# Attention in an encoder layer: two value products for a key tile instead of three, and the sum of the weights added up by DMA

## The chip, the cores and the metric

The kernel runs on one core of a Trainium2 chip. The metric is the time of one execution in microseconds (us). The engines are PE (TensorE, the matrix products), DVE (VectorE), ACT (ScalarE), POOL (GpSimd) and SP (SyncE, which here only issues DMAs). Each engine takes its instructions in the order of its own list and stops at one that has to wait. A DMA that POOL issues goes through the software queue (q0), one from SP through q1, one from ACT through q10; sixteen DMA engines serve all three.

## What is computed

One layer of a bidirectional encoder over a sequence of 2048 tokens and one of 256, with the same weights:

```
n = rmsnorm(x);  p = n @ w_in                          # projections of all mixers
m = mLSTM heads(p), both directions                    # 8 heads of 64
q, k = rope(rmsnorm(q)), rope(rmsnorm(k))              # 8 query heads, 2 key heads
o = softmax(q k^T / 8) v                               # each query sees its whole sequence
x = x + [m; o] @ w_out
x = x + (silu(g) * a) @ w_down,  [a; g] = conv3(rmsnorm(x) @ w_up)
y = rmsnorm(x)
```

The change lies in the line of the softmax. The kernel never normalizes the weights first: it takes w = exp(s - m) for a bound m of each query, sums w·v and w over the keys, and divides at the end.

All of it is float32. A fast product of PE takes operands rounded to a shorter form (the type F32R), so a number a is held as a1 + a2, a rounded part and what is left over, and a product a·b is made of a1·b1 + a1·b2 + a2·b1.

## The kernel before

Tokens stand in tiles of 128; the long sequence has 16 tiles, the short one 2. The program goes through a phase of projections, then attention and mLSTM together, then the output projection (phase C, `po` at L1001), which starts while attention still runs, then the convolution network. A generator for each of attention and mLSTM issues its work in small steps, and `run_both` draws from the one that is behind by a table of costs, so that PE gets both kinds mixed. The order on each engine is then set by the framework's scheduler, which places the instructions by its own times and by priorities; it isn't the order of the Python lines.

**Attention** works through 36 blocks (`hbs`): 32 of one head and 512 queries against the 16 key tiles of the long sequence, and 4 of two heads with 256 queries each against the 2 key tiles of the short one. A block goes through its key tiles two at a time (a pair, `kp`): 8 pairs in a large block, 1 in a small one, 260 in all. For a pair:

- `scores` (L577): four products of 512 columns give s - m for two key tiles in `ps`, a PSUM tile of two banks. ACT takes exp into `pe` (L587) and copies it rounded into the first half of `xx` (L588); DVE puts what is left over into the second half (L589).
- `values` (L592): for each of the two key tiles three products add up in one PSUM bank `pv`, with the keys on the contraction. L600 takes the rounded weights and `vv`, which holds the rounded values in columns 0 to 63 and ones in columns 64 to 127, so rows 64 to 127 of `pv` become the sum of the weights. L601 takes the rounded weights and `vl`, the left-over of the values, into rows 0 to 63. L602 takes the left-over of the weights and `vv`.
- Between pairs, `maxstep` (L548) makes products (`px`, L560) and a maximum on DVE (L562) for the next block's bound m.

After the last pair `fin1` (L604) has ACT copy the value rows of `pv` to `o` and the sum rows to `rs` (L612), and `fin2` (L614) has DVE take the reciprocal and multiply; POOL (SP for the last block) stores the result to `mix_d` (L624), from where phase C loads it (`cmx`, L971). The PSUM tiles `ps`, `px`, `pq` and `pr` share two buffers (tag "sc").

By the constants, `PLAG = 3` lets three pairs of scores be issued ahead of values, `XB = 4` pairs of weights (`xx`) and `PEB = 2` of `pe` have buffers.

**mLSTM on POOL.** POOL also serves mLSTM: it loads rows of gates by DMA (`dm`, L824), masks them (L828), scales keys (`kw`, L793, which the products `mu` of L806 take), and forms inverse roots (`mr`, L97, L98).

## Time and profile before

| what | value |
|---|---|
| median of three runs | 3317.9 us (3312.5 to 3319.42) |
| profiled execution, span from first to last instruction | 3315.5 us |
| attention's products, first scores to last values | 219.7 to 1756.3 us |
| PE busy in the span | 3240.5 us (98%) |
| mean granted clock of PE | 0.992 |
| DMA, mean share of the 16 engines from 222 to 1760 us | 0.38 |

The page gives the span of the profiled execution and no other time of it. A matrix product is in a pipeline, so its duration in a row is longer than the step from its start to the next product's start; what a product takes from PE is read from the starts. In a group's row, the figures behind the count are the group's busy time in us and the mean ns of one; behind the second bar stands how long its engine was idle just before, and what ended that. A row on DMAs gives the size of one and the median us from issue to landing.

### The profile page before, as it was taken

To read this page: it belongs to the slowest core of one execution; us is meant where nothing else is said; L and a number is where in the kernel's file an instruction comes from. 1 tells how busy PE (TensorE), PEld (TensorE's weight loads), DVE (VectorE), ACT (ScalarE), POOL (GpSimd) and SP (SyncE) were. 2 spreads that over 40 slices of the span, in tenths; PEclk is the share of its full clock that TensorE was granted. 3 is DMA by queue.
4 is the path that set the end of the run, shared out by engine and by line. 5 is a ranking of instruction groups with operands and counts; after the bars stand their busy time and mean duration, and the time that the engine had idled before them with its cause. 6 is when DMAs were issued, how large, how long until landed. Compare 5 with 4: busy or idle time off the path is not lost.

```text
span 3315.5 us, 53149 instructions
## 1 busy us (share of the span) xinstructions
PE 3240.5 (98%) x19488; PEld 3018.0 (91%) x19488; DVE 2429.5 (73%) x3759; ACT 1993.5 (60%) x3738; POOL 522.1 (16%) x917
## 2 busy tenths in 40 slices
PE   8989999999999999999999999999999999999998
PEld 7878888888888888788889999999999999999998
DVE  7755676676657768866666899998888889666654
ACT  5646666666675776655454555665676667454543
POOL 4561042223224323200000000000000000020101
PEclk9999999999999999999999999999999999999999
DMA  9973333343346444423227666767676567968663
GB/s 353 316 213 101 112 103 113 98 125 109 99 139 189 123 147 127 139 96 106 76 93 266 220 222 213 248 229 271 202 254 240 194 224 239 320 216 276 216 226 134
DMA packets 359117, 612.31 MB, mean 185 GB/s; under 512 B 31029, under 2 KB 215271, under 8 KB 358855
## 3 DMA queue, kind: packets, MB, share of 16 engines
q1 hardware_dynamic: 329431, 563.14, 50.5%
q0 software_dynamic: 11856, 33.96, 3.8%
q10 hardware_dynamic: 17568, 11.80, 1.1%
q8 instruction: 154, 2.52, 0.3%
q14 instruction: 108, 0.88, 0.1%
HBM read 444.85 MB, written 163.93 MB: 184 GB/s over the span
## 4 chain that ended last, share of the span: by engine, by line
PE 83%; issue 5%; DMA 4%; ACT 3%; DVE 3%; POOL 2%; SPq 1%; POOLq 0%; ACTq 0%; DVEq 0%
PE pa L1164 17%; PE pc L1164 8%; PE pf L1428 7%; PE po L1001 6%; PE pb L1164 4%; PE mj L720 4%; PE pj L238 4%; PE mv L730 4%; PE ph L1428 3%; PE ps L583 3%; PE pv L602 3%; PE pv L600 3%; PE ps L584 3%; PE pv L601 3%; PE px L560 3%
## 5 line engine op out<-in xcount | busy, mean ns | idle before, releaser
L589 DVE TENSOR_TENSOR xx<-pe,xx 128x1024 fp32r<-128x1024 f32 x260 | 319.0, 1227 | 171.4 <-ACT xx L588 169.9
L587 ACT ACTIVATE pe<-ps 128x1024 f32<-128x1024 f32 x260 | 266.1, 1024 | 231.8 <-PE ps L584 215.0
L562 DVE TENSOR_REDUCE mx<-px 128x1 f32<-128x1024 f32 x256 | 310.5, 1218 | 100.6 <-PE px L560 100.0
L588 ACT ACTIVATE xx<-pe 128x1024 fp32r<-128x1024 f32 x260 | 275.1, 1058 | 5.2 <-PE pv L602 0.2
L1381 POOL TENSOR_TENSOR sq<-sq,sq 128x384 f32<-128x384 f32 x38 | 48.5, 1277 | 1382.7 <-ACT sq L1377 1302.2
L1001 PEld LDWEIGHTS po<-cmx,wo 128*128 128x128 f32 x1728 | 229.9, 189 | 19.5 <-DVE cx L1008 1.1
L1001 PE MATMUL po<-cmx,wo 128*128 128x256 f32 x1728 | 238.7, 283 | 1.4 <-DVE cx L1008 1.0
L1168 ACT ACTIVATE u<-pa 128x386 f32<-128x386 f32 (+2 forms) x264 | 128.9, 489 | 173.9 <-PE pa L1164 168.7
L600 PE MATMUL pv<-xx,vv 128*128 128x512 f32 x520 | 212.4, 408 | 10.5 <-ACT rs L612 6.0
L583 PE MATMUL ps<-qq,kk 128*128 128x512 f32 x520 | 213.8, 411 | 8.2 <-ACT pe L587 3.9
L602 PE MATMUL pv<-xx,vv 128*128 128x512 f32 x520 | 211.0, 406 | 3.5 <-DVE xx L589 3.4
L584 PE MATMUL ps<-qm,kl 65*128 65x512 f32 x520 | 208.9, 402 | 0.0
L601 PE MATMUL pv<-xx,vl 128*64 128x512 f32 x520 | 207.3, 399 | 0.0
L720 PEld LDWEIGHTS mj<-mn,wm 128*128 128x128 f32 x1296 | 178.3, 193 | 18.3 <-ACT og L736 4.5
L720 PE MATMUL mj<-mn,wm 128*128 128x256 f32 x1296 | 189.6, 288 | 2.8 <-ACT og L736 2.8
L730 PE MATMUL mv<-wm,mn 128*128 128x256 f32 x1296 | 189.9, 286 | 1.3 <-ACT qb L726 1.3
L730 PEld LDWEIGHTS mv<-wm,mn 128*128 128x128 f32 x1296 | 176.1, 190 | 15.2 <-ACT qb L726 2.3
L238 PE MATMUL pj<-w_a,n1T 128*128 128x512 f32 (+1 forms) x864 | 167.8, 353 | 11.0 <-ACT w_a L105 7.1
L560 PE MATMUL px<-kk,qq 128*128 128x512 f32 x512 | 167.2, 408 | 2.4 <-ACT pe L587 2.4
L238 PEld LDWEIGHTS pj<-w_a,n1T 128*128 128x128 f32 x864 | 141.3, 192 | 30.6 <-ACT w_a L105 7.1
L1164 PE MATMUL pc<-nt,wb 128*128 128x386 f32 (+2 forms) x792 | 148.0, 341 | 0.0
L831 ACT ACTIVATE dm<-dm,tm 128x128 f32<-128x128 f32 x288 | 94.8, 392 | 86.0 <-POOL dm L828 85.7
(337 smaller groups left out, 8106.0 us busy)
## 6 DMA issues: line engine op xcount, KB each, us to landing
mn<-n_d SPq DMA_DIRECT2D x216, 256.0 KB, 3.1
ru<-w_up SPq DMA_DIRECT2D x88, 512.0 KB, 5.1
rs<-wsu_d SPq DMA_DIRECT2D x88, 512.0 KB, 5.7
...
re_t<-wsd_d SPq DMA_DIRECT2D x45, 512.0 KB, 5.4
wsu_d<-tw SPq DMA_DIRECT2D x44, 512.0 KB, 4.2
...
```

Of the source, the lines that this page charges most:

```text
L238: nc.tensor.matmul(pjs[t][:, c0:c1], nTs[tiles[t]][:, c, a, :], ws[c][:, b, c0:c1], start=(c == 0 and k == 0), stop=(c == NCC - 1 and k == 2))
L562: nc.vector.tensor_reduce(s.mx[:, t0, z0:z0 + 1], ps, AX.X, ALU.max)
L583: nc.tensor.matmul(o, kk[:, kc:kc + P], s.qq, start=True, stop=False)
L584: nc.tensor.matmul(o, kl1[:, kc:kc + P], s.qm, start=False, stop=True)
L589: nc.vector.tensor_tensor(x[:, 1], pe, f32(x[:, 0]), ALU.subtract)
L600: nc.tensor.matmul(s.pv, vv[:, kt % 4, :], x1, start=kt == 0, stop=False)
L602: nc.tensor.matmul(s.pv, vv[:, kt % 4, :], x2, start=False, stop=kt == s.nk - 1)
L720: nc.tensor.matmul(pj[:, o].rearrange("p (n t) -> p n t", t=P), s.w[c][:, a, o * P:(o + 1) * P], nT[c][:, :, h, :], start=(c + o + k == 0) ...
L730: nc.tensor.matmul(pv[:, o], nT[c][:, o, a, :], s.w[c][:, h, 256:512], start=(c + o + k == 0), stop=(c == NCC - 1 and k == 2 and o == 1))
L1001: nc.tensor.matmul(po[:, o], wo[c][z // 2][:, a, n], mx[c][:, h, :], start=c + o + k == 0, stop=c == NCC - 1 and o == 1 and k == 2)
L1164: s.nc.tensor.matmul(p, w[:, aa, c, :], ops[k][:, c, bb, 0:s.n], start=c == 0 and i == 0 and not add, stop=c == NCC // 2 - 1 and i == 2, s ...
L1428: nc.tensor.matmul(ps[c], w[:, aa, c, :], t[:, gi - g0, bb, 0:H], start=gi == 0 and m == 0 and not more, stop=gi == NG - 1 and m == 2, ski ...
```

## The change

The value tile `vv` now holds the rounded values in columns 0 to 63 and their left-over in columns 64 to 127, without ones. One product with the rounded weights gives both parts, in rows 0 to 63 and 64 to 127 of `pv`; a second, with the left-over of the weights and the rounded values, adds to rows 0 to 63. The two halves are added in `fin1`. The sum of the weights is no longer made by these products: the first pair's exp goes into a tile of its own, `acc`, and each later pair's `pe` is added to it by a DMA (L603), which POOL issues one pair later; a last DMA (L610) adds the tile's right half to its left half. `fin2` splits that half, `fin3` sums it over the keys with two products against a tile of ones (L651), and `fin4` divides. These steps wait in a list (`later`, `step`) for some pairs. The buffers change: `XB` 4 to 2, `PEB` 2 to 3, `PLAG` 3 to 1, `acc` has two, `o1` two.

```diff
--- before.py
+++ after.py
@@ -1,3 +1,4 @@
+import itertools
 from contextlib import ExitStack
 
 import numpy as np
@@ -69,9 +70,9 @@
 RW = 4
 PO = 4
 PB = 4
-PEB = 2
-XB = 4
-PLAG = 3
+PEB = 3
+XB = 2
+PLAG = 1
 ZT = 3
 SG = 3
 RS = 2
@@ -480,20 +481,17 @@
             s = f"{n}_{t0}"
             kk = sp.tile([P, m * P], F32R, tag="kk" + s, name=f"kk{grp}_{s}", bufs=1)
             kl1 = sp.tile([65, m * P], F32R, tag="kl1" + s, name=f"kl1{grp}_{s}", bufs=1)
-            vv = sp.tile([P, m, P], F32R, tag="vv" + s, name=f"vv{grp}_{s}", bufs=1)
-            vl = sp.tile([P, m, HD], F32R, tag="vl" + s, name=f"vl{grp}_{s}", bufs=1)
+            vv = sp.tile([P, m, 2, HD], F32R, tag="vv" + s, name=f"vv{grp}_{s}", bufs=1)
             c = slice((k0 + t0) * P, (k0 + t0 + m) * P)
             if after is not None:
-                for t in (kk[0:1, 0:1], kk[HD:HD + 1, 0:1], kl1[0:1, 0:1], vv[0:1, 0, 0:1], vl[0:1, 0, 0:1]):
+                for t in (kk[0:1, 0:1], kk[HD:HD + 1, 0:1], kl1[0:1, 0:1], vv[0:1, 0, 0, 0:1]):
                     nc.gpsimd.tensor_copy(t, after[0:1, 0:1])
-            nc.gpsimd.memset(f32(vv[:, :, HD:P]), 1.0)
             for r in (0, HD):
                 nc.gpsimd.dma_start(f32(kk[r:r + HD, :]), g.k_d[grp, 0:HD, c])
             nc.gpsimd.dma_start(f32(kl1[0:HD, :]), g.k_d[grp, HD:P, c])
             nc.gpsimd.memset(f32(kl1[64:65, :]), 1.0)
-            for a, t in ((0, vv[:, :, 0:HD]), (1, vl)):
-                nc.gpsimd.dma_start(f32(t), g.v_d[grp, :, k0 + t0:k0 + t0 + m, a])
-            parts.append((kk, kl1, vv, vl))
+            nc.gpsimd.dma_start(f32(vv), g.v_d[grp, :, k0 + t0:k0 + t0 + m])
+            parts.append((kk, kl1, vv))
 
     class HB:
         pass
@@ -574,6 +572,17 @@
                              stop=True)
         nc.scalar.activation(s.qm[HD:HD + 1, 0:s.N], pr[HD:HD + 1, 0:s.N], AF.Copy)
 
+    due, now, count = [], [0], itertools.count()
+
+    def later(n, f):
+        due.append((now[0] + n, next(count), f))
+        due.sort(key=lambda v: v[:2])
+
+    def step():
+        while due and due[0][0] <= now[0]:
+            due.pop(0)[2]()
+        now[0] += 1
+
     def scores(s, kp):
         kk, kl1 = s.kv[kp // 2][0:2]
         ps = pp.tile([P, 1024], F32, tag="sc", name=f"ps{s.nm}_{kp}")
@@ -582,36 +591,70 @@
             o = ps[:, z * 512:(z + 1) * 512]
             nc.tensor.matmul(o, kk[:, kc:kc + P], s.qq, start=True, stop=False)
             nc.tensor.matmul(o, kl1[:, kc:kc + P], s.qm, start=False, stop=True)
-        pe = sp.tile([P, 1024], F32, tag="pe", name=f"pe{s.nm}_{kp}", bufs=PEB)
+        if kp:
+            pe = sp.tile([P, 1024], F32, tag="pe", name=f"pe{s.nm}_{kp}", bufs=PEB)
+        else:
+            pe = s.acc = sp.tile([P, 1024], F32, tag="acc", name="acc" + s.nm, bufs=2)
         x = sp.tile([P, 2, 1024], F32R, tag="px", name=f"xx{s.nm}_{kp}", bufs=XB)
         nc.scalar.activation(pe, ps, AF.Exp)
         nc.scalar.activation(x[:, 0], pe, AF.Copy)
         nc.vector.tensor_tensor(x[:, 1], pe, f32(x[:, 0]), ALU.subtract)
+        if kp:
+            later(1, lambda: nc.gpsimd.dma_start(s.acc, pe, accum_op=ALU.add))
+        if kp == s.nk // 2 - 1:
+            lo, hi = s.acc[:, 0:512], s.acc[:, 512:1024]
+            n = 2 if kp else 1
+            if s.last:
+                later(n, lambda: nc.vector.tensor_tensor(lo, lo, hi, ALU.add))
+            else:
+                later(n, lambda: nc.gpsimd.dma_start(lo, hi, accum_op=ALU.add))
+            for k, f in enumerate((fin2, fin3, fin4)):
+                later(2 * n + k, lambda f=f: f(s))
         return kp, x
 
     def values(s, kp, x):
 
         if kp == 0:
             s.pv = pp.tile([P, 512], F32, tag="pv", name="pv" + s.nm, bufs=1)
-        vv, vl = s.kv[kp // 2][2:4]
+        vv = s.kv[kp // 2][2]
         for z in range(2):
             kt = 2 * kp + z
             x1, x2 = (x[:, a, z * 512:(z + 1) * 512] for a in range(2))
-            nc.tensor.matmul(s.pv, vv[:, kt % 4, :], x1, start=kt == 0, stop=False)
-            nc.tensor.matmul(s.pv[0:HD], vl[:, kt % 4, :], x1, start=False, stop=False)
-            nc.tensor.matmul(s.pv, vv[:, kt % 4, :], x2, start=False, stop=kt == s.nk - 1)
+            for a in (0, 1) if z == 0 else (1, 0):
+                if a:
+                    nc.tensor.matmul(s.pv[0:HD], vv[:, kt % 4, 0], x2, start=False, stop=False)
+                else:
+                    nc.tensor.matmul(s.pv, vv[:, kt % 4].rearrange("p a d -> p (a d)"), x1, start=kt == 0,
+                                     stop=kt == s.nk - 1)
 
     def fin1(s):
 
-        s.o1 = sp.tile([P, 256], F32, tag="o1", name="o1" + s.nm, bufs=1)
+        s.o1 = sp.tile([P, 256], F32, tag="o1", name="o1" + s.nm, bufs=2)
+        o2 = sp.tile([P, 256], F32, tag="o2", name="o2" + s.nm, bufs=1)
         if s.n == len(hbs) - 3:
             g.hold = s.o1
+        for z in range(2):
+            r, c = slice(HD * z, HD * z + HD), slice(256 * z, 256 * z + 256)
+            nc.scalar.activation(o2[r], s.pv[HD:P, c], AF.Copy)
+            nc.vector.tensor_tensor(s.o1[r], s.pv[0:HD, c], o2[r], ALU.add)
+
+    def fin2(s):
+
+        s.ah = sp.tile([P, 2, 512], F32R, tag="ah", name="ah" + s.nm, bufs=1)
+        nc.scalar.activation(s.ah[:, 0], s.acc[:, 0:512], AF.Copy)
+        nc.vector.tensor_tensor(s.ah[:, 1], s.acc[:, 0:512], f32(s.ah[:, 0]), ALU.subtract)
+
+    def fin3(s):
+
+        ps = pp.tile([P, 1024], F32, tag="sc", name="pa" + s.nm)
+        for a in range(2):
+            nc.tensor.matmul(ps[:, 0:512], g.onesr, s.ah[:, a], start=a == 0, stop=a == 1)
         s.rs = sp.tile([P, 256], F32, tag="rs", name="rs" + s.nm, bufs=1)
         for z in range(2):
-            for r, o in ((0, s.o1), (HD, s.rs)):
-                nc.scalar.activation(o[HD * z:HD * z + HD], s.pv[r:r + HD, 256 * z:256 * z + 256], AF.Copy)
-
-    def fin2(s):
+            r, c = slice(HD * z, HD * z + HD), slice(256 * z, 256 * z + 256)
+            nc.scalar.activation(s.rs[r], ps[r, c], AF.Copy)
+
+    def fin4(s):
         for t in range(2):
             c = slice(t * P, (t + 1) * P)
             nc.vector.reciprocal(s.rs[:, c], s.rs[:, c])
@@ -634,14 +677,13 @@
         yield 0.5
     prep2(cur)
     load_kv(0, 0, NT1, cur.m4)
-    pend, fins = [], []
+    pend = []
 
     def drain():
         b, kp, x = pend.pop(0)
         values(b, kp, x)
         if kp == b.nk // 2 - 1:
             fin1(b)
-            fins.append(b)
 
     for n in range(len(hbs)):
         nxt = prep(n + 1) if n + 1 < len(hbs) else None
@@ -650,7 +692,6 @@
         nkp = cur.nk // 2
         for kp in range(nkp):
             pend.append((cur, *scores(cur, kp)))
-            ready = bool(fins)
             if len(pend) > PLAG:
                 drain()
             if nxt is not None and nxt.todo:
@@ -658,8 +699,7 @@
                     maxstep(nxt)
                 if not nxt.todo:
                     prep2(nxt)
-            if ready:
-                fin2(fins.pop(0))
+            step()
             yield 2.3
         if nxt is not None and nxt.todo:
             while nxt.todo:
@@ -669,8 +709,8 @@
     while pend:
         drain()
         yield 1
-    for b in fins:
-        fin2(b)
+    while due:
+        step()
 
 
 def mlstm(g, tc, s1, sp, sw, sn, pj_, pm):
@@ -1520,6 +1560,8 @@
             sm2 = pool(s_m, "m_o", bufs=2, side="right")
             pm = pool(s_m, "m_p", bufs=MB, space=PSUM, side="right")
             sk = pool(s2, "b_k", bufs=1)
+            g.onesr = sk.tile([P, P], F32R, name="onesr")
+            nc.gpsimd.memset(f32(g.onesr), 1.0)
             sa = pool(s2, "b_s", bufs=2)
             pa = pool(s2, "b_p", bufs=SCB, space=PSUM)
```

The order on POOL, inside mLSTM's second round (`dm` gates, `mr` inverse roots, `kw` scaled keys, `qb` and `va` memsets). Before:

```order
L624 DMA mix_d<-o_0_4739 64x256 [waits DMASW5_49,DVE_49]
L624 DMA mix_d<-o_0_4739 64x256
L824 DMA dm_8_5901<-nm_d 128x512 [waits PE_49]
L828 AFFINE_SELECT dm_8_5901<-dm_8_5901 128x256 [waits DMASW7_49]
L828 AFFINE_SELECT dm_8_5901<-dm_8_5901 128x256
L824 DMA dm_9_6152<-nm_d 128x512 [waits DMASW0_49,DVE_49,PE_49]
L97 TENSOR_SCALAR mr_5_5769<-mms_5_5766 128x2 [waits Activation_49]
L98 TENSOR_TENSOR mr_5_5769<-mr_5_5769,mhalf 128x2 [waits Pool_49]
L828 AFFINE_SELECT dm_9_6152<-dm_9_6152 128x256 [waits DMASW0_49]
L828 AFFINE_SELECT dm_9_6152<-dm_9_6152 128x256
L836 DMA ogr_10_6294<-og_d 128x256 [waits DMAHW7_49,DVE_49]
L725 MEMSET qb_3_4906 64x2x128 [waits PE_49]
```

Now (`acc` is the tile of sums, `pe` a pair's weights):

```order
L603 DMA acc_4_4672<-pe_4_4_4942 128x1024 [waits DMASW1_49,Activation_49]
L864 DMA dm_12_6667<-nm_d 128x512 [waits DMASW3_49,DVE_49,PE_49]
L603 DMA acc_4_4672<-pe_4_5_4988 128x1024 [waits DMASW2_49,Activation_49]
L868 AFFINE_SELECT dm_12_6667<-dm_12_6667 128x256 [waits DMASW3_49]
L868 AFFINE_SELECT dm_12_6667<-dm_12_6667 128x256
L667 DMA mix_d<-o_0_4681 64x256 [waits DVE_49]
L667 DMA mix_d<-o_0_4681 64x256
L98 TENSOR_SCALAR mr_9_6533<-mms_9_6530 128x2 [waits Activation_49]
L99 TENSOR_TENSOR mr_9_6533<-mr_9_6533,mhalf 128x2 [waits Pool_49]
L777 MEMSET va_3_4907 128x4
L833 TENSOR_TENSOR kw_4_6441<-mkt_2_6439,tm 128x256 [waits PE_49]
L876 DMA ogr_14_7085<-og_d 128x256 [waits DMAHW2_49,DVE_49]
```

Two of a block's seven additions stand among mLSTM's steps here; each waits for ACT and for a DMA semaphore of the software queue (DMASW), and the steps behind it are issued after it.

The order on PE around one pair of a large block (`ps` scores, `pv` values, `px` next block's bound, `mv`, `mN`, `mT`, `mt` mLSTM). Before:

```order
L730 MATMUL mv_1_5615<-wm_5_4843,mn_1_5_5549 128x256
L600 MATMUL pv_4_4768<-xx_4_3_4764,vv_16_4_2556 128x512
L601 MATMUL pv_4_4768<-xx_4_3_4764,vl_16_4_2557 64x512
L730 MATMUL mv_1_5615<-wm_5_4843,mn_1_5_5549 128x256
L730 MATMUL mv_1_5615<-wm_6_4844,mn_1_6_5550 128x256 x4
L863 MATMUL mN_7_6122<-va_3_2386,dm_7_5783 128x65 x4
L602 MATMUL pv_4_4768<-xx_4_3_4764,vv_16_4_2556 128x512
L600 MATMUL pv_4_4768<-xx_4_3_4764,vv_16_4_2556 128x512
L601 MATMUL pv_4_4768<-xx_4_3_4764,vl_16_4_2557 64x512
L602 MATMUL pv_4_4768<-xx_4_3_4764,vv_16_4_2556 128x512
L730 MATMUL mv_1_5615<-wm_6_4844,mn_1_6_5550 128x256
L583 MATMUL ps_4_5_4978<-qq_4_4164,kk_16_8_2570 128x512
```

Now:

```order
L592 MATMUL ps_4_4_4937<-qq_4_4169,kk_16_8_2561 128x512
L593 MATMUL ps_4_4_4937<-qm_4_4171,kl_16_8_2562 128x512
L592 MATMUL ps_4_4_4937<-qq_4_4169,kk_16_8_2561 128x512
L593 MATMUL ps_4_4_4937<-qm_4_4171,kl_16_8_2562 128x512
L627 MATMUL pv_4_4720<-xx_4_3_4768,vv_16_4_2551 128x512
L558 MATMUL px_4_2_1_4951<-kk_16_8_2561,qq_4_4662 128x512
L558 MATMUL px_4_2_1_4951<-kk_16_12_2573,qq_4_4662 128x512
L827 MATMUL mt_2_6436<-ident,mkT_2_4902 128x128 x2
L925 MATMUL mT_2_6511<-ident,hh_4_5521 128x128
L925 MATMUL mT_2_6511<-ident,hh_5_5777 128x128
L625 MATMUL pv_4_4720<-xx_4_3_4768,vv_16_4_2551 64x512 x2
L627 MATMUL pv_4_4720<-xx_4_3_4768,vv_16_4_2551 128x512
```

The six value products of a pair, in a group of two and one of four, have become four, in a group of one and one of three; the group of one stands right behind the next pair's scores.

The order on PE behind the last block's values, where phase C's products (`po`) follow. Before:

```order
L600 MATMUL pv_12_19545<-xx_12_7_19739,vv_16_12_10502 128x512
L601 MATMUL pv_12_19545<-xx_12_7_19739,vl_16_12_10503 64x512
L602 MATMUL pv_12_19545<-xx_12_7_19739,vv_16_12_10502 128x512
L1001 MATMUL po_3_20177<-cmx_3_19887,wo_1_17024 128x256 x3
L1001 MATMUL po_3_20177<-cmx_4_19891,wo_1_17050 128x256 x3
L1001 MATMUL po_3_20177<-cmx_5_19895,wo_1_17060 128x256 x3
```

Now (`pa` sums the weights with ones):

```order
L1041 MATMUL po_3_20215<-cmx_3_19929,wo_1_17054 128x256 x3
L1041 MATMUL po_3_20215<-cmx_4_19933,wo_1_17079 128x256 x3
L1041 MATMUL po_3_20215<-cmx_5_19937,wo_1_17089 128x256 x3
L1041 MATMUL po_3_20215<-cmx_6_19941,wo_1_17140 128x256 x3
L1041 MATMUL po_3_20215<-cmx_7_19945,wo_1_17150 128x256 x3
L1041 MATMUL po_3_20215<-cmx_0_19916,wo_1_17009 128x256 x3
L1041 MATMUL po_3_20215<-cmx_1_19921,wo_1_17019 128x256 x3
L1041 MATMUL po_3_20215<-cmx_2_19925,wo_1_17044 128x256 x3
L651 MATMUL pa_12_19853<-ah_12_19850,onesr 128x512 [waits Activation_49]
L1041 MATMUL po_3_20215<-cmx_3_19929,wo_1_17054 128x256 x3
L1041 MATMUL po_3_20215<-cmx_4_19933,wo_1_17079 128x256 x3
L651 MATMUL pa_12_19853<-ah_12_19850,onesr 128x512 [waits DVE_49]
```

Behind the last values phase C's products follow as before; the two products for the sum of the last block's weights, which wait for ACT and DVE, now stand among them, 26 and 32 products behind the last value product.

## The prediction

> **What bounds the kernel now.** I read the head of the page, then the busy times of the stretch that holds attention, then PE in order of time, then the groups with the idle time before them.
>
> ```profile
> span 3315.5 us, 53149 instructions
> 222.00:1760.00 1538.00, 1504.87 (x9468) 1308.97 (x9468) 1048.33 (x1851) 965.31 (x2035) 347.14 (x677) 1.00 0.38 118
> ```
>
> The second row is the stretch from 222 to 1760 us: its length, then busy time of PE, PE's weight loads, DVE, ACT and POOL, then PE's clock (1.00), the share of the DMA engines (0.38) and GB/s. PE is busy 98% of it, DVE 68%, ACT 63%, POOL 23%. A busy PE need not be a full one, since products overlap in its pipeline; so the starts count:
>
> ```profile
> 1743.18 0.40 PE L602 MATMUL pv<-xx,vv 128*128 128x512 f32 x1
> 1743.41 0.39 PE L600 MATMUL pv<-xx,vv 128*128 128x512 f32 x1
> 1743.64 0.40 PE L601 MATMUL pv<-xx,vl 128*64 128x512 f32 x1
> 1743.88 0.39 PE L602 MATMUL pv<-xx,vv 128*128 128x512 f32 x1
> ...
> 1746.69 0.40 PE L601 MATMUL pv<-xx,vl 128*64 128x512 f32 x1
> ```
>
> From the first of these rows to the last are 15 steps from one product of 512 columns to the next, in 3.51 us: 0.234 us a step. The product with 64 output rows (L601) takes the same step as the others (1743.64 to 1743.88). Next, whether PE waits for what it takes:
>
> ```profile
> L583 PE MATMUL ps<-qq,kk 128*128 128x512 f32 x520 | 213.8, 411 | 8.2 <-ACT pe L587 3.9 <-DVE mx L562 2.5 <-ACT qm L575 1.7
> L600 PE MATMUL pv<-xx,vv 128*128 128x512 f32 x520 | 212.4, 408 | 10.5 <-ACT rs L612 6.0 <-ACT xx L588 4.1
> L602 PE MATMUL pv<-xx,vv 128*128 128x512 f32 x520 | 211.0, 406 | 3.5 <-DVE xx L589 3.4
> L560 PE MATMUL px<-kk,qq 128*128 128x512 f32 x512 | 167.2, 408 | 2.4 <-ACT pe L587 2.4
> L601 PE MATMUL pv<-xx,vl 128*64 128x512 f32 x520 | 207.3, 399 | 0.0
> L583 PEld LDWEIGHTS ps<-qq,kk 128*128 128x128 f32 x520 | 98.9, 190 | 29.1 <-ACT pe L587 7.1 <-DVE mx L562 5.4 <-ACT qm L575 2.0
> ```
>
> Attention's products were held 8.2 + 10.5 + 3.5 + 2.4 = 24.6 us in all, in 1538, and none of that by POOL or a DMA. So PE's own work sets the time here, and work taken from PE is worth its steps as long as nobody else becomes late.
>
> The Trainium skill (Trainium Kernel Development and Optimization, Best Practices) calls matmul busy time a bad measure and the busy share of weight loads a good one. By that share, 1309 of 1538 or 85%, PE would have 15% to spare, and if as much of the removed work came out of spare time the saving would shrink by some 16 us. The starts above show products without a gap, at a step longer than a weight load (0.19 us, the last row), so I keep the full step.
>
> **The change part by part.**
>
> *Products.* The 520 products of L601 go: 520 x 0.234 = 121.7 us off PE. The 36 blocks each get two products of 512 columns for the sum of the weights: 72 x 0.234 = 16.8 us on. The other value products keep their number and their columns. Net: -104.9 us, or 0.40 us of a pair's 1538/260 = 5.92 us. A pair then has 5.51 us, a large block of eight pairs 44.1 us.
>
> *ACT and DVE.* The nearest rows for the added work:
>
> ```profile
> L1136 ACT ACTIVATE wd<-ru 128x512 fp32r<-128x512 f32 x66 | 41.0, 623 | 0.0
> L1137 DVE TENSOR_TENSOR wd<-ru,wd 128x512 fp32r<-128x512 f32 x66 | 45.3, 687 | 1.2 <-ACT wd L1136 1.2
> L618 DVE TENSOR_TENSOR o<-o,rs 128x256 f32<-128x256 f32 x36 | 15.0, 418 | 0.3
> ```
>
> ACT splits the sums once a block, 36 x 0.62 = 22 us, and has as many copies out of PSUM as before (two from `pv`, two from `pa`, where it had four from `pv`). DVE gets the left-over of that split, 36 x 0.69 = 25 us, and two additions of the value halves, 72 x 0.42 = 30 us. Over the shortened stretch of 1433 us DVE rises to 1103/1433 = 77% and ACT to 987/1433 = 69%. That lies beside PE's work, but PE now has less to do while it waits for them, and the free share of DVE falls from 32% to 23%. The halving of the buffers of `xx` comes on top. The rows on the order show that PE already took values about one pair behind scores, so `PLAG` itself moves little there. The 24.6 us of waits may stay or take back all 105; I let them nearly double, +22 us, since nothing in the stretch is close to full.
>
> *The additions.* 32 large blocks get seven additions of 512 KB and all but the last block one of 256 KB: 224 + 35 = 259 issues on POOL.
>
> ```profile
> L624 POOL DMA_DIRECT2D mix_d<-o x70 | 38.6, 554 | 355.8 <-ACT xx L588 171.0 <-issue 71.1 <-ACT csq L1011 35.2
> mix_d<-o POOLq DMA_DIRECT2D x70, 64.0 KB, 2.3
> ogr<-og_d POOLq DMA_DIRECT2D x27, 128.0 KB, 2.9
> dm<-nm_d POOLq DMA_DIRECT2D x72, 256.0 KB, 3.7
> rd<-w_down SPq DMA_DIRECT2D x22, 512.0 KB, 3.3
> ```
>
> At 0.554 us an issue POOL gets 143 us more, 490 of 1433 us or 34%. The weight lies elsewhere: the additions of a block go into one tile, so each waits for the landing of the one before, and POOL waits with it. Before has no adding DMA, and none within the chip's own memory. From the rows of POOL's queue, 128 KB more cost 0.8 us, so 512 KB would land after 3.7 + 2 x 0.8 = 5.3 us. From below, SP's row of 512 KB has 3.3. From above, if reading the target costs as much again as reading the source, 5.3 + 4 x 0.8 = 8.5. I take 5.3: it is the row of the same queue carried to this size, with the second read hidden, and it lies between. A block's chain is then 7 x 5.3 + 0.55 for the next issue = 37.7 us; the last addition of 256 KB goes beside the next block's first. That is under 44.1, and `pe` has three buffers, so exp of a pair need not wait until two pairs later. The chain is hidden, with 15% to spare.
>
> The Trainium skill (DMA: Bandwidth & Descriptors, Anatomy of one DMA — SWDGE (gpsimd) path) fits a DMA of this queue as 2.0 us plus its bytes at 436 GB/s, and (Collectives: The Full Stack, The bandwidth ceiling: the fold count and why AG ≠ RS ≠ AR) says that an add must read two sources through one ring. An estimate from both is 2.0 + 2 x 1.2 = 4.4 us, by which the sum would lose only its term for the end, 5 us. The trace's 256 KB row has 3.7 where the fit gives 2.6, so here the queue is slower than the page.
>
> *What waits behind an addition on POOL.* In the order, masks of `dm`, the keys `kw` and the roots `mr` stand behind additions.
>
> ```profile
> POOL dm L828 <- DMA dm<-nm_d: 188.7, 66, 5.1
> POOL kw L793 <- PE mu L806: 169.5, 45, 21.1
> ```
>
> POOL spent 189 us waiting for `dm` to land and 170 for PE to free `kw`, so it ran ahead of PE, with room to be late. A chain of 37.7 us in 44.1 uses up much of this room; `dm` itself now lands behind 512 KB on the same queue. What is late next is `mu` (L806), which takes `kw`, and PE stops there. Nothing (if the room suffices) up to the whole of the rival below; I take 0.3 us a block, +10 us.
>
> *Stores, loads, the end.* Ten loads and ten memsets of the value tiles are saved on POOL, off any path. `fin4` comes some pairs later, so phase C gets `mix_d` later; other tiles cover that until the last block:
>
> ```profile
> 1700.00:1760.00 60.00, 13.73 (x14) 0.97 0.19 60
> ...
> 1756.30 0.39 PE L602 MATMUL pv<-xx,vv 128*128 128x512 f32 x1
> 1756.54 16.21 PE L1001 MATMUL po<-cmx,wo 128*128 128x256 f32 x135
> ```
>
> (the first row counts 14 exps of ACT in 60 us.) There a pair takes 4.3 us, 3.9 after the change, less than an addition's 5.3: the chain falls behind by up to 7 x 1.4 = 10 us. Before, 135 products of phase C followed the last values at 0.12 us each. Now the sum's products stand 26 products, 3.1 us, behind them. Of the 10 us I charge 5; between nothing and, at 8.5, 7 x 4.6 = 32.
>
> *The sum*, on the profiled execution: 3315.5 - 121.7 + 16.8 + 22 + 10 + 5 = 3247.6. The median of the runs stands 2.4 us above that span, so **3250 us**.
>
> **The rivals.**
>
> *The additions set the pace (slower).* Place: POOL, from one addition of a block to the next. As soon as an addition takes over (44.1 - 0.55)/7 = 6.2 us, exp finds no free `pe`, ACT stops, and scores stop behind it; above 6.7 us the saving of 3.3 us a block is gone. For it: the DMA engines already carry 38%, the second read may not hide, mLSTM's waits on POOL add to the chain. Against it: 5.3 from the rows. At 7 us a block takes 49.6, and 32 x (49.6 - 44.1) = 176 us come back: 3315.5 - 104.9 + 176 + 2.4 = 3389; at 8.5 it is 3723.
>
> *The saving goes into waits for ACT and DVE (no change).* With two buffers of `xx`, a late left-over on DVE stops values on PE and the copy on ACT at once. It needs 0.4 us more wait a pair, against 0.1 now: about 3318. Against it: DVE and ACT stay under 80%.
>
> *All of it is kept.* No added wait anywhere: 3315.5 - 104.9 + 2.4 = 3213. Against it: fewer buffers and fuller engines.
>
> **How the numbers follow.** The forecast gets 0.58, all kept 0.08, no change 0.10, the additions' pace 0.24. A measurement of this kernel tells about 0.2% (6.6 us) from no change. Faster: 0.58 + 0.08 = 0.66; the case of no change gives 0.09 to within 0.2% and 0.01 to slower, which makes 0.25. The forecast's own range is 3215 to 3295. For 8 times in 10 the range must take in no change and the near part of the slow rival, an addition of up to about 6.8 us: 3208 to 3350, with 0.03 below and some 0.15 above.
>
> **What would show it right or wrong.** The rows of L603 should land after 4 to 6 us. PE's starts in a pair should keep 0.234, with four value products a pair, and idle time before PE's attention groups near 45 us. PE should not wait for POOL, and ACT's exp not for a DMA. The stretch from first scores to last values should shrink from 1538 to about 1470 us. Landings over 6.2 us, with exp waiting for L603, would be the slow rival; waits of values for DVE of 100 us the second. The stages before 222 us and after phase C should keep their times; a difference there would be something I did not see.

## The result: 8.7% slower, and the profile after

The change takes 3604.4 us in the median of four runs (3596.9 to 3607.0), the kernel before 3317.6 us beside it: a ratio of 1.0866, with a 95% interval of 1.0851 to 1.0882. The forecast was 3250 us. The profiled execution has a span of 3603.0 us, 287.5 more than before.

First the stretch from the first scores to the last values, in the view of busy times by window (length; then busy time of PE, its weight loads, DVE, ACT, POOL; PE's clock, DMA share, GB/s). Before, cut at its last value product:

```profile
222.00:1757.00 1535.00, 1501.87 (x9442) 1305.97 (x9442) 1046.67 (x1849) 964.07 (x2032) 347.14 (x677) 1.00 0.38 118
```

After:

```profile
222.00:2032.00 1810.00, 1534.07 (x8997) 1313.33 (x8996) 1099.87 (x1953) 990.21 (x2067) 550.58 (x916) 0.90 0.69 169
```

The stretch is 275 us longer. PE's idle time in it rose from 1535 - 1502 = 33 to 1810 - 1534 = 276 us, which is 243 more. PE's busy time rose too, by 32 us, though 104.9 us of products were taken from it. The clock column says why: 1.00 before, 0.90 now, so each product takes longer on average; that is worth 32 + 105 = 137 us, an estimate from the two busy times and the prediction's net work. So -105 us of work, +243 of idle time and +137 of lower clock make +275. The other 12 us lie behind the stretch (1571 us after its end, 1558.5 before).

What ended PE's idle time, by groups of instructions:

```profile
L592 PE MATMUL ps<-qq,kk 128*128 128x512 f32 x518 | 228.3, 441 | 33.2 <-ACT pe L599 18.4 <-DVE mx L560 7.6 <-ACT rs L655 6.2
L627 PE MATMUL pv<-xx,vv 128*128 128x512 f32 x520 | 219.4, 435 | 38.3 <-ACT xx L600 33.7 <-DVE o L639 2.9 <-DMA mn<-n_d 1.4
L558 PE MATMUL px<-kk,qq 128*128 128x512 f32 x512 | 183.3, 441 | 71.7 <-ACT pe L599 41.3 <-DVE mx L560 26.7 <-ACT acc L599 1.9
L625 PE MATMUL pv<-xx,vv 128*64 128x512 f32 x520 | 181.4, 427 | 15.7 <-DVE xx L601 15.7
```

PE idles 159 us ahead of these four, 25 ahead of the four of before, and mostly for exp (`pe`) and its rounded copy (`xx`), both on ACT. Neither ACT nor DVE is fuller than before (ACT 990 of 1810 us). So the next question is what stands ahead of exp. The waits of ACT in the stretch, after:

```profile
ACT dm L871 <- POOL dm L868: 186.9, 57, 10.1
ACT pe L599 <- PE ps L593: 161.2, 109, 6.8
ACT ah L644 <- DMA acc<-acc: 116.6, 28, 13.2
ACT qm L573 <- PE pr L571: 68.1, 19, 7.6
ACT cmx L1012 <- DMA cmx<-mix_d: 53.2, 17, 10.2
...
ACT pe L599 <- DMA acc<-pe: 4.6, 2, 3.1
```

and the first two of before:

```profile
ACT pe L587 <- PE ps L584: 214.7, 131, 6.7
ACT dm L831 <- POOL dm L828: 85.7, 57, 4.8
```

ACT waits twice as long for POOL's masks (`dm`), up to 10.1 us at a time; for the last landing of a block's sum before it may split it (`ah`, new, up to 13.2 us); and for `cmx` (13.2 us before). Exp comes behind these in ACT's own order and is late with them, although exp itself hardly waits for a landing (4.6 us). POOL's waits, after:

```profile
POOL acc L603 <- ACT pe L599: 283.8, 67, 10.2
POOL acc L603 <- DMA acc<-pe: 192.3, 50, 7.0
POOL dm L868 <- DMA dm<-nm_d: 119.6, 47, 6.6
POOL acc L610 <- DMA acc<-pe: 103.8, 26, 6.8
```

This view puts 284 us of POOL's waits at additions down to an exp and 192 + 104 us to a landing. But it names whatever last updated one of the semaphores waited for, and ACT updates its own with most of its instructions (1297 of 2066 in the stretch), so an exp can be named by coincidence. The trace has the times to check it: the end of the exp whose weights an addition takes, and the landing of the addition before it. Measured so, 124 of the waits ahead of L603, 509 us together, end about 0.5 us after that landing, and only 64, 262 us, right after the addition's own exp. Of the waits ahead of L610, 124 us end with a landing. POOL thus stands still for landings more than twice as long as for exp. The landings themselves (KB each, median us from issue to landing):

```profile
acc<-pe POOLq DMA_DIRECT2D x224, 512.0 KB, 5.2
dm<-nm_d POOLq DMA_DIRECT2D x72, 256.0 KB, 5.2
acc<-acc POOLq DMA_DIRECT2D x35, 256.0 KB, 3.7
mix_d<-o POOLq DMA_DIRECT2D x70, 64.0 KB, 4.7
```

An addition lands after 5.2 us in the median, where 5.3 was forecast; the mean is 5.5. But the gates `dm` now take 5.2 us (3.7 before) and the stores of `mix_d` 4.7 (2.3 before). They share POOL's queue with the additions, which is only part of the reason: with as many stores going through ACT's queue instead (a run below) they still take 4.5 and 2.8 us.

One block's end shows the whole chain in order of time (start, duration, engine; in brackets the engine's idle time and what ended it):

```profile
1551.75 0.92 POOL L603 DMA_DIRECT2D acc<-pe  x1 [4.05 <-issue]
...
1556.87 0.87 POOL L603 DMA_DIRECT2D acc<-pe  x1 [4.20 <-DMA acc<-pe]
...
1559.06 3.13 PE L1041 MATMUL po<-cmx,wo 128*128 128x256 f32 x25
1562.35 0.85 POOL L610 DMA_DIRECT2D acc<-acc  x1 [4.60 <-DMA acc<-pe]
1566.97 0.63 ACT L644 ACTIVATE ah<-acc 128x512 fp32r<-128x512 f32 x1 [11.58 <-DMA acc<-acc]
...
1568.03 1.02 ACT L599 ACTIVATE pe<-ps 128x1024 f32<-128x1024 f32 x1
...
1569.52 1.22 PE L558 MATMUL px<-kk,qq 128*128 128x512 f32 x2 [7.33 <-DVE mx L560]
```

The block's last two additions and the half addition follow each other by their landings; ACT stops 11.58 us at the split; the next pair's exp, whose scores were issued from 1558 us on, starts at 1568.03; PE has nothing left at 1562.2 and idles 7.33 us. The seven additions of this block began at 1517.87 and the last had landed at 1562.06, after 44 us, where 37.7 were forecast. Three of its earlier additions, and the exp whose weights the last of these takes, show why:

```profile
1531.16 0.86 POOL L603 DMA_DIRECT2D acc<-pe  x1 [4.23 <-ACT xx L600]
...
1533.06 1.03 ACT L599 ACTIVATE pe<-ps 128x1024 f32<-128x1024 f32 x1 [0.26 <-PE ps L593]
...
1539.44 0.86 POOL L603 DMA_DIRECT2D acc<-pe  x1 [7.43 <-issue]
...
1545.74 0.86 POOL L603 DMA_DIRECT2D acc<-pe  x1 [5.43 <-ACT pe L599]
```

The addition at 1545.74 takes weights that were ready at 1534.09; the exp that the view names is a later pair's. By the trace, the addition before it landed at 1544.91. None of this block's seven additions waited for its own exp, which was done 2.5 to 11.7 us ahead: the landings took 4.5 to 7.7 us each, 39.2 us together, and each next start came 0.5 to 2 us behind a landing. The last landing is 14 us behind the block's last exp.

Over all 32 large blocks a chain took 48.3 us in the mean (36.7 to 59.4). Of these, 38.8 us are the seven landings, 3.2 us the half microsecond that lies between a landing and the next addition's start, and 6.4 us later starts, 5.1 of them until the addition's own exp was done.

What follows for PE, in three windows around the same place:

```profile
1562.00:1569.00 7.00, 0.19 (x2) 0.00 (x0) 1.37 (x2) 1.98 (x4) 0.85 (x1) 0.68 0.48 126
1569.00:1573.00 4.00, 3.48 (x9) 2.60 (x10) 3.94 (x8) 3.35 (x9) 0.86 (x1) 0.50 0.60 115
1573.00:1585.00 12.00, 12.00 (x81) 11.17 (x80) 7.00 (x11) 3.87 (x5) 1.56 (x2) 0.93 0.37 89
```

For 4 us behind the idle time the granted clock is 0.50. So this wait is paid for twice. The Trainium skill (TensorE: Matmul & The Clock Gate, What's actually happening) says that the gate passes all or half of the pulses and falls to half after an idle window of some 3.4 us; the 0.50 here agrees.

A second path, through the store of `mix_d`:

```profile
1696.92 0.86 POOL L603 DMA_DIRECT2D acc<-pe  x1 [4.16 <-issue]
1697.45 1.41 POOL L667 DMA_DIRECT2D mix_d<-o  x2
1702.23 0.80 SPq L1011 DMA_DIRECT2D cmx<-mix_d  x2
1704.67 0.83 ACT L1012 ACTIVATE cmx<-cmx 128x256 fp32r<-128x256 f32 x2 [10.14 <-DMA cmx<-mix_d]
...
1705.13 1.26 PE L1041 MATMUL po<-cmx,wo 128*128 128x256 f32 x4 [9.29 <-ACT cmx L1012]
...
1705.52 1.03 ACT L599 ACTIVATE pe<-ps 128x1024 f32<-128x1024 f32 x1
```

The store stands behind an addition on POOL, the load of `cmx` behind the store, ACT behind the load for 10.14 us, and exp behind ACT.

### The profile page after: what moved, and what is told of

Its sections match the earlier page's. It is cut to its first block, busy times and chain, and to the rows that moved or that the text cites. A ratio compares the mean times of both kernels' runs of the same rounds, so it can differ in the third digit from the quotient of the medians.

```text
span 3603.0 us, 53035 instructions
## 1 busy us (share of the span) xinstructions
PE 3276.9 (91%) x19040; PEld 3029.1 (84%) x19040; DVE 2483.6 (69%) x3868; ACT 2017.4 (56%) x3774; POOL 724.6 (20%) x1153
## 5 line engine op out<-in xcount | busy, mean ns | idle before, releaser
L601 DVE TENSOR_TENSOR xx<-pe,xx 128x1024 fp32r<-128x1024 f32 x224 | 275.2, 1230 | 178.5 <-ACT xx L600 170.7
L603 POOL DMA_DIRECT2D acc<-pe x224 | 200.5, 895 | 799.1 <-ACT pe L599 283.8
L599 ACT ACTIVATE pe<-ps 128x1024 f32<-128x1024 f32 x224 | 229.2, 1024 | 167.9 <-PE ps L593 161.2
L627 PE MATMUL pv<-xx,vv 128*128 128x512 f32 x520 | 219.4, 435 | 38.3 <-ACT xx L600 33.7
L558 PE MATMUL px<-kk,qq 128*128 128x512 f32 x512 | 183.3, 441 | 71.7 <-ACT pe L599 41.3
L600 ACT ACTIVATE xx<-pe 128x1024 fp32r<-128x1024 f32 x224 | 236.4, 1057 | 16.6 <-PE pv L627 7.8
L760 PE MATMUL mj<-mn,wm 128*128 128x256 f32 x1296 | 206.5, 306 | 19.2 <-ACT og L776 9.8
L625 PE MATMUL pv<-xx,vv 128*64 128x512 f32 x520 | 181.4, 427 | 15.7 <-DVE xx L601 15.7
L627 PEld LDWEIGHTS pv<-xx,vv 128*128 128x128 f32 x520 | 106.1, 204 | 79.8 <-ACT xx L600 44.2
L558 PEld LDWEIGHTS px<-kk,qq 128*128 128x128 f32 x512 | 92.8, 208 | 94.1 <-ACT pe L599 48.9
```

The costliest lines, as they stand in the source:

```text
L558: nc.tensor.matmul(ps[:, z * 512:(z + 1) * 512], s.qq[:, t0 * P:(t0 + 1) * P], s.kv[2 * z0 + z][0], start=True, stop=True)
L599: nc.scalar.activation(pe, ps, AF.Exp)
L600: nc.scalar.activation(x[:, 0], pe, AF.Copy)
L601: nc.vector.tensor_tensor(x[:, 1], pe, f32(x[:, 0]), ALU.subtract)
L627: nc.tensor.matmul(s.pv, vv[:, kt % 4].rearrange("p a d -> p (a d)"), x1, start=kt == 0, stop=kt == s.nk - 1)
L760: nc.tensor.matmul(pj[:, o].rearrange("p (n t) -> p n t", t=P), s.w[c][:, a, o * P:(o + 1) * P], nT[c][:, :, h, :], start=(c + o + k == 0) ...
```

## The experiments

Ratios are against the kernel before on the same chip, with 95% intervals; a hundredth is 33 us, and a difference of two ratios is known to within some 7 to 12 us. Each run was made from the changed kernel unless it says otherwise. The diffs are shortened to the lines that matter. Where a run leaves out a part of the sums, it also adds a small constant so that the division stays finite. In the runs with additions later, two chains, sums set aside, and POOL emptied, the split's tile `ah` also takes a buffer of `pe`.

**The buffers alone** (in the kernel before):

```diff
-PEB = 2; XB = 4; PLAG = 3
+PEB = 3; XB = 2; PLAG = 1
```

> The kernel before with the change's buffers and lag alone: PEB 3, XB 2, PLAG 1; three products a key tile as before, no additions. Theory A: 3310 to 3350 us. Rival B: 3450 us or more.

3333.3 us, 1.006 [1.0037, 1.0083]. Fewer buffers cost some 19 us with three products; they are not the cause.

**The products alone** (in the kernel before; the sum of the weights is left out, and DVE adds the value halves as in the change):

```diff
-            nc.tensor.matmul(s.pv, vv[:, kt % 4, :], x1, ...)
-            nc.tensor.matmul(s.pv[0:HD], vl[:, kt % 4, :], x1, ...)
-            nc.tensor.matmul(s.pv, vv[:, kt % 4, :], x2, ...)
+            nc.tensor.matmul(s.pv, vv[:, kt % 4].rearrange("p a d -> p (a d)"), x1, ...)
+            nc.tensor.matmul(s.pv[0:HD], vv[:, kt % 4, 0], x2, ...)
```

> Left out: the sum of the weights (no additions, no split, no products with ones; the division takes another row of the value products instead). This is the kernel before with two value products a key tile in place of three and with its own four buffers of xx and values up to three pairs behind: what the removed products alone are worth. Theory 3 (the smaller buffers take the saving: with two buffers of xx values wait for the left-over and PE falls under its full clock): with the deep buffers 104 to 122 us are kept, 3195 to 3225 us, PE's clock 0.99. Theory 4 (PE waits for ACT and DVE whatever the buffers, so the removed work was not worth its steps): 3290 to 3340 us.

> The same with the change's buffers: two of xx, three of pe, values one pair behind. Left out as there: the sum of the weights. Theory 3: 3310 to 3340 us, as the change without its additions (3336). Theory 4: the same as with the deep buffers within 25 us. If it is faster than 3300, the split and the products with ones cost more than I think.

> The same with three buffers of xx, two of pe and values two pairs behind, the sum of the weights left out again. Theory 3: between the two others, 3220 to 3280 us. Theory 4: no difference among the three.

With before's buffers 3266.2 us, 0.9863 [0.9845, 0.9880]; with the change's 3276.4, 0.9893 [0.9877, 0.9909]; with three of `xx` 3260.9, 0.9847 [0.9828, 0.9866]. Neither theory had the times: the three differ by 5 to 16 us, so the buffers matter little, as theory 4 had it; but 35 to 50 us are saved, neither 104 to 122 nor next to nothing. The stretch of the first:

```profile
222.00:1708.00 1486.00, 1417.10 (x8922) 1231.08 (x8923) 1066.09 (x1919) 948.77 (x1959) 335.33 (x655) 0.98 0.40 121
```

Against before, PE's work fell by 122 us and its busy time by 85 (the clock, 0.98, takes 37), and its idle time rose by 36, from 33 to 69. Ahead of attention's products PE now idled 47 us, not 24.6, and nearly all of it ended with an instruction of ACT or DVE: given less to do, PE waits for these two sooner. That the clock fell because of this idle time is a reading, not shown by a run of its own.

**The change without its additions, and with their traffic alone:**

```diff
-            later(1, lambda: nc.gpsimd.dma_start(s.acc, pe, accum_op=ALU.add))
-                later(n, lambda: nc.gpsimd.dma_start(lo, hi, accum_op=ALU.add))
# the second kernel also:
+            nc.scalar.dma_start(g.junk_d[kp], pe)
```

> Left out: all adding DMAs, so the sum of the weights is that of a block's first pair alone; a small constant is added to it so that the division stays finite. Everything else is as in the change, the split, the products with ones and the smaller buffers too. If the additions and the waits for their landings are what costs (theory 1: the two queues that must keep their order, POOL's with the chain of additions and ACT's with the split that waits for the last landing), the time falls to 3220 to 3270 us, the stretch from 222 us on to some 1450 us and PE's clock there is back at 0.99. If something else in the change costs (two buffers of xx, values one pair behind, the sums of value halves on DVE), it stays above 3400 us.

> Left out: the additions, as in the kernel without them; instead ACT's queue stores every pe tile but a block's first to the chip's memory, 224 stores of 512 KB, which nobody reads and for which only the reuse of pe waits. So much of the additions' traffic is there without their order: no chain, no wait on POOL, no split that waits. Theory 1: within 40 us of the kernel without additions, and under 3310 us. Theory 2 (traffic slows loads and stores that others wait for): 3400 us or more.

3335.6 us, 1.0059 [1.0044, 1.0074], and 3343.1 us, 1.0084 [1.0066, 1.0102]. The first lies between its two forecasts (3220 to 3270, or above 3400); the second is within 40 us of it, as theory 1 had it, but not under 3310. Two things follow. The additions cost 1.0866 - 1.0059 = 0.081, 268 us; and without them the change is still slower than before. The kernel with the same products and buffers but no split, no products with ones and no late end stood at 0.9893: these three cost 0.017, 55 us, where 16.8 had been charged for the products of ones. And 224 stores of 512 KB for which only the reuse of `pe` waits cost 8 us, hardly more than the two intervals allow for: traffic of this size is not the cause. These stores read the weights but not the sums, and go through ACT's queue, so what an addition does to POOL's own queue isn't in this run. The stretch without additions, and three windows in it:

```profile
222.00:1778.00 1556.00, 1460.89 (x8987) 1259.80 (x8988) 1096.91 (x1955) 992.62 (x2065) 348.43 (x656) 0.96 0.38 115
```

```profile
1571.00:1575.00 4.00, 0.67 (x4) 0.23 (x3) 4.00 (x6) 0.00 (x0) 0.00 (x0) 0.70 0.75 235
1575.00:1590.00 15.00, 14.74 (x41) 10.66 (x41) 5.17 (x9) 8.44 (x12) 1.09 (x2) 0.51 0.21 61
1590.00:1600.00 10.00, 6.92 (x21) 4.49 (x20) 7.40 (x8) 4.02 (x6) 0.00 (x0) 0.83 0.00 0
```

Here PE idled 95 us in the stretch, and the clock was 0.96. PE's rows where these windows begin:

```profile
1570.32 0.68 PE L621 MATMUL pv<-xx,vv 128*64 128x512 f32 x2 [2.05 <-DVE xx L601]
1570.85 0.63 PE L623 MATMUL pv<-xx,vv 128*128 128x512 f32 x2
1574.80 1.11 PE L621 MATMUL pv<-xx,vv 128*64 128x512 f32 x2 [3.33 <-DVE xx L601]
```

Two waits of 2.05 and 3.33 us are followed by 15 us at half clock, though PE is busy in 14.74 of them. The Trainium skill (TensorE: Matmul & The Clock Gate, What's actually happening) has the full clock back after one busy window of 3.4 us; this place doesn't agree, and the measurement decides.

**Half of each addition:**

```diff
-dma_start(s.acc, pe, accum_op=ALU.add)
+dma_start(s.acc[:, 0:512], pe[:, 0:512], accum_op=ALU.add)
```

> The change with additions of half the size: each of the seven adds only the left 512 columns, so the even key tiles alone are summed (and a small constant is added ahead of the reciprocal). Same count, same chain, half the bytes. If the chain of landings decides, a landing falls from 5.2 to about 3.7 us, a block from 56 us by 7 x 1.5 = 10 us or more, 3250 to 3350 us. If it is POOL's waits as such, whatever their length: 3450 us or more. Rival B: about 3600.

3450.2 us, 1.0408 [1.0378, 1.0438]. This is not the 3250 to 3350 us forecast for the case that the chain of landings decides, but the edge of the other case, that POOL's waits cost as such. Still, the landings take 3.7 us instead of 5.2, POOL's waits that end with a landing ahead of L603 fall from 509 to 230 us by the trace's times, and the cost of the additions falls from 268 to 116 us. So more than half of it goes with the size of an addition, most likely through the length of its landing; 116 us stay with landings this short.

**The split later, and the additions later:**

```diff
# split, products with ones and division three pairs later
-                later(2 * n + k, lambda f=f: f(s))
+                later(2 * n + k + (3 if kp else 0), lambda f=f: f(s))
# the other kernel: additions two pairs later, four buffers of pe, split two pairs later still
-            later(1, lambda: nc.gpsimd.dma_start(s.acc, pe, accum_op=ALU.add))
+            later(2, lambda: nc.gpsimd.dma_start(s.acc, pe, accum_op=ALU.add))
```

> The split, the products with ones and the division of a large block come three pairs later; the additions are untouched, the result is the reference's. Theory 1a (ACT stops at the split until the half addition has landed, 117 us in 28 waits of up to 13 us, and exp stands behind it): those waits go, and with them PE's long idle times and part of the half clock behind them; 3400 to 3480 us. Theory 1b (the chain of additions on POOL alone makes masks, roots and stores late): 3560 to 3610 us. Theory 2 (the traffic of the additions slows every transfer): 3580 to 3610 us.

> Additions are issued two pairs later instead of one, with four buffers of pe instead of three, the half addition one pair later and the split two more pairs behind it (its tile takes a buffer of pe); the result is the reference's. Theory 1 (POOL stops at an addition whose exp is not yet done, 284 us in 67 waits, and ACT at a split whose sum has not landed): both waits go, 3300 to 3420 us. If POOL's stop for exp costs nothing, it is as with the late split alone. Theory 2 (traffic): 3560 us or more.

3570.4 us, 1.0771 [1.0755, 1.0787], and 3528.7 us, 1.0638 [1.0616, 1.0660]. The late split was placed later by the program, yet ACT's waits at it did not shrink (144 us in 31 waits), so it tests its theory only weakly. With the additions later, ACT's waits for a landing at the split did go, from 117 to 15 us. POOL's wait for exp fell from 284 to 144 us by the view (262 to 133 by the trace's times). That for landings rose from 192 us by the view (509 to 578 by the trace's times):

```profile
POOL acc L603 <- DMA acc<-pe: 287.5, 68, 8.2
```

A part of POOL's wait moved from one cause to the other; 76 us were gained, less than the 180 us or more of the forecast.

**Two chains:**

```diff
-dma_start(s.acc, pe, accum_op=ALU.add)
+dma_start(s.acc2 if kp % 2 else s.acc, pe, accum_op=ALU.add)   # joined by one more addition
```

> The change with two tiles of sums, one for even and one for odd pairs, which a last addition joins, so that an addition waits only for the one before the last; the split comes later (its tile takes a buffer of pe). The result is the reference's. Theory 1b (each addition waits on POOL for the landing before it, 197 us, and what stands behind is late): those waits go, 3400 to 3500 us. If POOL's order against ACT's exp is what costs, or the traffic, it stays at 3540 to 3610 us.

3492.7 us, 1.0548 [1.0527, 1.0569]: 105 us gained, as theory 1b had it. POOL's wait for the landing before fell from 192 to 20 us (by the trace's times, from 509 to 4), but 147 us of waiting now lie ahead of the addition that joins the tiles and 116 ahead of the half addition. A new wait came in on ACT too, at the next block's second pair, whose exp needs the second tile back:

```profile
POOL acc L605 <- DMA acc<-pe: 20.1, 6, 4.6
ACT acc L601 <- DMA acc<-acc: 105.0, 23, 10.1
```

**The additions set aside**, into a tile that nobody reads:

```diff
-dma_start(s.acc, pe, accum_op=ALU.add)
+dma_start(g.ad, pe, accum_op=ALU.add)
```

> Left out: the additions go into a tile of their own that nobody reads, so the sum of the weights is that of a block's first pair alone (with a small constant added). POOL issues every addition, the half addition too, in its place and waits as in the change; what falls away is only that ACT's split and the next use of the sums' tile wait for a landing. Without any addition the time is 3336, with all 3604. Theory 1a (ACT's stop at the split is the larger part): 3340 to 3420 us. Theory 1b (POOL's own order, with masks, roots and stores late, is the larger part): 3480 to 3570 us.

3571.4 us, 1.0784 [1.0752, 1.0817]: 240 of the 268 us stay, just above what theory 1b expected. ACT's stop for the sums, plain as it is in the timeline, is worth 27 us alone; 30 us of stops at the split stay in this run, for the buffer of `pe` that its tile takes, so this figure is rather low. The other stops are larger than in the change (187, 94 and 53 us there):

```profile
ACT dm L871 <- POOL dm L868: 210.1, 60, 12.0
DVE hh L917 <- POOL mr L99: 113.4, 44, 7.3
ACT cmx L1012 <- DMA cmx<-mix_d: 69.1, 29, 9.6
```

**The removed work given back:**

```diff
-                    nc.tensor.matmul(s.pv[0:HD], vv[:, kt % 4, 0], x2, ...)
+                    for _ in range(2):
+                        nc.tensor.matmul(s.pv[0:HD], vv[:, kt % 4, 0], x2, ...)
```

> The change with 520 more value products: the product of the weights' left-over is issued twice, so that left-over counts double. PE gets back 520 x 0.234 = 122 us of work, nothing else changes. If PE's work still sets the time in the change: 3690 to 3730 us. Theory 5 (in the change PE stands behind ACT and POOL, and its idle time and its half clock swallow the saving): under 3650 us, with less idle time and a higher clock in the stretch than the 0.90 of the change.

3622.5 us, 1.0928 [1.0906, 1.0949]: 122 us of products cost 18 to 21 us.

```profile
222.00:2056.00 1834.00, 1615.29 (x9518) 1358.81 (x9516) 1103.36 (x1950) 989.63 (x2062) 554.97 (x913) 0.94 0.69 166
```

PE idles 219 us in place of 276 and its clock rises from 0.90 to 0.94. In the change PE's work does not set the time: of work given back, a sixth shows.

**Other adders**: POOL itself, DVE, and DVE for pairs with three DMAs a block:

```diff
# POOL; for DVE nc.vector
-later(1, lambda: nc.gpsimd.dma_start(s.acc, pe, accum_op=ALU.add))
+later(1, lambda: nc.gpsimd.tensor_tensor(s.acc, s.acc, pe, ALU.add))
# pairs: pe1 onto acc by DVE; pe2+pe3, pe4+pe5, pe6+pe7 by DVE, then
+later(1, lambda: nc.gpsimd.dma_start(s.acc, b, accum_op=ALU.add))
```

> The change with every addition made by POOL itself (one instruction over 128 x 1024 in place of a DMA). From 1.28 us for 384 columns an addition takes about 3.4 us; POOL gets 35 + 224 x 3.4 = 800 us of work and no landing to wait for. Theory A: POOL's chain is 7 x 3.4 = 24 us a block, well under 44, so 3230 to 3320 us. Rival B: 3450 us or more. If an addition on POOL slows beside DVE to over 6 us: 3500 or more.

> No adding DMA: DVE adds each pair's weights to the sums, 224 x 1.23 = 276 us, and the halves. The result is the reference's. POOL and ACT wait for no landing. DVE then has some 1380 of 1480 us. If being nearly full is enough to stop PE: 3420 to 3520 us, with values waiting for the left-over on DVE. If DVE keeps up: 3340 to 3380 us. Theory 1 excludes only 3560 and more.

> Three adding DMAs a large block instead of seven: DVE adds the second pair's weights to the sums and joins the others two by two (four additions of 1.2 us), and a DMA adds each joined pair; split, products with ones and division one or two pairs later. The result is the reference's. Theory 1 (the cost goes with the number of landings and stops on POOL): a bit under half of the 269 us of the additions stays, 3400 to 3470 us, if DVE (then some 87% busy) does not stop PE itself; otherwise 3480 to 3550 us.

POOL: 3486.1 us, 1.0516 [1.0486, 1.0547]. DVE: 3418.0, 1.0308 [1.0285, 1.0331]. Pairs: 3456.5, 1.0437 [1.0404, 1.0470]. The first was a miss for theory A, and another cause came in; the third is as theory 1 had it. Additions on POOL, and DVE's left-over beside them:

```profile
L603 POOL TENSOR_TENSOR acc<-acc,pe 128x1024 f32<-128x1024 f32 x224 | 557.9, 2491 | 391.8 <-ACT pe L599 349.3 <-DVE xx L601 20.0 <-DVE C L857 10.3
L601 DVE TENSOR_TENSOR xx<-pe,xx 128x1024 fp32r<-128x1024 f32 x224 | 392.1, 1753 | 112.4 <-ACT xx L600 111.8
```

An addition takes 2.49 us on POOL, and DVE's subtraction rises from 1.23 to 1.75 us; PE's waits for it ahead of L625 rise from 15.7 to 58.5 us. The Trainium skill (GPSIMD Engine Reference, Key points) says that POOL shares its interfaces to SBUF with DVE, with contention when a DVE instruction has two inputs there. The row agrees. With DVE adding, no landing is waited for, and of the additions' 268 us 83 remain: DVE is then busy 1359 of 1638 us, and values wait for it (36.7 us on PE). The time lies at the lower end of the 3420 to 3520 us expected if a nearly full DVE stops PE. Three DMAs a block instead of seven, with their work on DVE, leave 125. None of these comes near the kernel before.

**POOL emptied of mLSTM's work**, with the additions, without them, and with two chains:

```diff
-        nc.gpsimd.dma_start(o.dm..., g.nm_d[...])          # og too
+        nc.sync.dma_start(o.dm..., g.nm_d[...])
-            nc.gpsimd.affine_select(out=o.dm[:, d], ...)
+            nc.vector.tensor_tensor(o.dm[:, d], o.dm[:, d], g.mask[:, d], ALU.add)
-            nc.gpsimd.tensor_tensor(kw, ...)
+            nc.vector.tensor_tensor(kw, ...)
```

> The change with most of mLSTM's work taken off POOL: the gate rows and the output gates are loaded by SP, DVE adds a mask that was made once, DVE scales the keys; POOL keeps the additions, the stores and the inverse roots. The result is the reference's. Theory 1b (what stands behind the additions on POOL is late, and ACT and DVE stop for it): the waits of ACT for masks go (187 us in the change), 3400 to 3500 us. Rival (the chain of landings itself holds exp and the split, whatever else POOL does): 3560 to 3610 us.

> The same moves off POOL without any addition (left out: the additions, so the sum of the weights is that of a block's first pair alone, with a small constant added). It tells what the moves alone do: against the kernel without additions (3336 us) both theories expect 3320 to 3370 us, since ACT's 94 us of waits for masks may shrink and DVE gets 72 masks and 72 scaled keys more, about 80 us of its work. What lies between this run and the one with additions is then the cost of the additions with POOL nearly to themselves: theory 1b 60 to 150 us, the rival 200 us or more.

> The same moves off POOL with the two tiles of sums. The result is the reference's. If both causes are what the runs so far say (work behind the additions on POOL, and each addition's wait for the landing before it), their gains add up in part: 3380 to 3440 us. If the moves bring nothing, 3490 us as with two tiles alone. None of the theories expects a time under that of the kernel before.

3483.1 us, 1.0505 [1.0488, 1.0521]; without additions 3330.0, 1.0044 [1.0029, 1.0059]; two chains 3491.2, 1.0533 [1.0498, 1.0568]. The moves alone do nearly nothing (1.0059 to 1.0044), but with them the additions cost 1.0505 - 1.0044 = 0.046, 153 us, not 268. So 115 us of the additions' cost went through mLSTM's steps that stand behind them on POOL, or through its loads, which no longer take POOL's queue; the run doesn't tell these two apart. On POOL itself the waits for landings ahead of L603 stay (648 us by the trace's times). With both, 3380 to 3440 us were forecast, so that was a miss: the gains of the moves and of the two chains do not add up; with both, ACT still waits 104 us for a join. How the last 153 us divide among the chain's waits, the late `cmx` (76 us on ACT there) and the split was not settled.

## Why the prediction was wrong, step by step

*What bounds the kernel now.* Right for the kernel before. But "work taken from PE is worth its steps as long as nobody else becomes late" is where the saving ended: with the products removed and little else changed, 45 us came of 121.7. In the stretch the loss was 73 us: 36 of new idle time and 37 of clock. The rule on weight loads of the Trainium skill (Trainium Kernel Development and Optimization, Best Practices), set aside since the starts showed no gap, would have taken off some 16 us. It pointed the right way, but fell short. The rival in which the saving goes into waits for ACT and DVE gave 3318 us; without the additions the change takes 3336. That rival was the better forecast of that part.

*ACT and DVE.* The +22 us for doubled waits: without the additions PE idled 95 us in the stretch, 62 more than before, and the lower clock took another 64 (1460.9 busy against 1501.9 - 104.9 = 1397). The two make 126 us, five to six times the term, and half of that is the lower clock, which the prediction put at nothing.

*The additions.* The median landing was right, 5.2 us for 5.3. The step that failed is "The chain is hidden, with 15% to spare". A block's chain took 48.3 us in the mean, not 37.7: the mean landing is longer than the median, half a microsecond lies between a landing and the next start, and some starts were late. Even without the late starts it is 42.0 us, and that would have left 5% of the 44.1, not 15. Above all, the step compared the chain's length with the block's, as if POOL had nothing else in its list. In fact POOL stands still for 509 us of landings and 262 us of exps ahead of the additions, and masks, roots and stores wait behind these. ACT stops for them, and exp, which hardly waits for a DMA itself (4.6 us in all), stands behind them on ACT. A late exp can make the next addition late in turn: so the traces read, and the runs show the sum of this, not each link of it.

*What waits behind an addition on POOL.* The place was named, and the price, 10 us, was the error. Setting the sums aside left 240 of 268 us, so most of it lies on POOL's side, in its order or its queue; taking mLSTM's steps and loads off POOL took 115 of it away. The 189 and 170 us that POOL spent waiting in the kernel before were read as room. They were waits for landings and for PE at particular places, and in the change 120 and 46 us of them are still there.

*The end.* 5 us were charged; 12 us more lie behind the stretch.

*The rivals.* The slow one had the right side and the right engine, but its point (a landing over 6.2 us, exp without a free `pe`) was not reached: exp waited 4.6 us for landings, and the loss came at landings of 5.2 us in the median. "All of it is kept" is excluded by the products alone.

*What would show it.* Landings of 4 to 6 us: seen. Four value products a pair: seen; a step of 0.234 us only while the clock is full. Idle time near 45 us: 159 in the four groups. PE not waiting for POOL and exp not for a DMA: both nearly true, and no proof of health, since the waits go through instructions that stand ahead. The stretch at 1470 us: 1810.

In sum, from the ratios: products -45 us, smaller buffers +10, split with products of ones and late end +55, additions +268; that makes 288. These are steps from run to run that end at the change, so they must add up to the 287 measured; that they do is no further proof.
